# Moving the start addresses of staged weights and activations in one fp32r network kernel

## The chip, the cores and the metric

One core of one Trainium2 chip runs the whole program. The metric is the device time of one execution in microseconds; of several runs the median is given, with the lowest and the highest.

## What is computed

Two network blocks of two layers each, on 256 tokens of width 1024, all in float32. Cut to the part that the change touches most, a layer of the second block is

```
h = rmsnorm(x, norm1_g[l])
z = h @ w_in[l]                      # projections of four attentions, and 4 x 1024 gates
o = four attentions of z             # each 256 wide
lifted = einsum('bsnc,ncd->bsnd', branches, w_branch[l])
mixed = sum(sigmoid(z_gate) * lifted, over the four)
x = x + mixed @ w_out[l]
h2 = rmsnorm(x, norm2_g[l])
x = x + square(relu(h2 @ w_up[l])) @ w_down[l]      # w_up 1024 x 4096
```

The first block has a layer with attention and pooling and a layer with a gated convolution, each followed by a mixture of 16 experts. A final norm ends the program.

## The kernel before

**Products.** Activations lie transposed in SBUF: 128 features on the partitions, 256 tokens along the free dimension. A product of full precision is built from three fp32r products: a tensor is held as a high part and a low part, and `mm3` (L160 to L163) issues the high weights times the high activations (L161), the high weights times the low activations (L162) and the low weights times the high activations (L163). Each of the three loads its own 128x128 weight tile (a row LDWEIGHTS, on the weight-load side of TensorE) and then streams 256 columns (a row MATMUL). The weight load of the next product overlaps the streaming of this one.

**Staging.** Weights come by DMA as 1 MB chunks `w`. `half` (L132 to L137) takes half a chunk and has ScalarE write its high part `whi` (L133) and VectorE its low part `wlo` (L134), each 128x1024 floats, into a staging pool. The pools stand in a list and are taken in turn: `stage` alone in the first block, `stage` and `stage_b` in the second block, `stage`, `stage_b` and `ml` during its feed-forward. So one half chunk feeds 24 products in a row (8 tiles of 128 columns, three products each), and the next 24 read their weights from the next pool of the list.

**The streamed operands.** `feature_linear` (48 products, two half chunks) streams `a` in the first block, `act` (the normed x, L1100) for the projections and gates of the second, `mx` (the mixed gates) for `w_out`, and the tag `oT` for the feed-forward's `up`. `lift` streams `oT`, the attentions' outputs. `down` streams `hid`, the squared relu, and adds into four PSUM accumulators `d`. The feed-forward has 16 steps; step cj issues `up(cj + 1)` and then `down(cj)`.

**Where tiles begin.** A pool is a stretch of each partition's SBUF, and a tile begins where the tiles allocated before it in its pool end. So an extra tile ahead of others moves all that follow. The program before has one such tile already: `gap`, 32 floats (L1632), in the pool `ml` ahead of the buffers of `hid`.

**Order.** Each engine has its own instruction stream, in an order that a scheduler sets when the program is built. VectorE (DVE) computes in its stream the low parts of the weights, the low parts of activations, the residual adds, the masks and the softmax pieces. The branch of the fourth attention finds its largest scores with eight rounds of MAX and MATCH_REPLACE for each of two token blocks (L1369 to L1373), through a small tile `m8`.

Of the kernel before, what the change touches and what calls it, by code (L numbers as in the profile page):

```python
# [10 lines left out]
F32 = mybir.dt.float32  # L11
# [10 lines left out]
NK = 8  # L22
# [38 lines left out]
def build(tc, I, O):  # L61
    nc = tc.nc
    V, A, G, T = nc.vector, nc.scalar, nc.gpsimd, nc.tensor
    es = ExitStack()
    with es:
        const = es.enter_context(tc.tile_pool(name="const", bufs=1))
        ring = es.enter_context(tc.tile_pool(name="ring", bufs=4))
        stage = es.enter_context(tc.tile_pool(name="stage", bufs=1))
        psum = es.enter_context(tc.tile_pool(name="psum", bufs=1, space=PSUM))

        def acc(name="acc"):
            return psum.tile([128, 512], F32, name=name, tag="acc", bufs=2)

# [16 lines left out]
        def C(name):  # L90
            if name in C1T:
                a, n = C1T[name]
                return cst1[:, a:a + n]
            a, n = CT[name]
            return cst[:, a:a + n]
# [5 lines left out]
        b1 = ExitStack()  # L101
        c1 = b1.enter_context(tc.tile_pool(name="c1", bufs=1))
        ring_b = b1.enter_context(tc.tile_pool(name="ring_b", bufs=7))
        pb = c1.tile([128, NPB], F32, name="pb")
        cst1 = c1.tile([128, NC1], F32, name="cst1")

# [2 lines left out]
            return pb[:, a:a + n]  # L109

        ident, ones = C("ident"), C("ones")
        epst = const.tile([128, 16], F32, name="epst")[:, 0:1]
        V.memset(epst, EPS)
        identb, causal, cmpm, hsel = cb[:, 0:128], cb[:, 128:256], cb[:, 256:286], cb[:, 286:798]

# [49 lines left out]
        def pair(shape, name, pool, bufs=1):  # L165
            return (pool.tile(shape, F32R, name=name + "h", tag=name + "h", bufs=bufs),
                    pool.tile(shape, F32R, name=name + "l", tag=name + "l", bufs=bufs))

        def token_linear(name, j0, a, done, ncol=512, alloc=acc, between=lambda: None, need=None):

            blocks = (0, 1)
# [29 lines left out]
        def feature_linear(name, j, a):  # L201

            w = chunk2(name, j)
            ps = acc("fm")
            for mm in range(2):
                for k in range(NK):
                    mm3(ps[:, S * mm:S * mm + S], tile_of(w[mm], k), pick(a, lambda z: z[:, k]),
                        k == 0, k == NK - 1)
            return ps
# [147 lines left out]
        class Conditions:  # L357
# [3 lines left out]
            def __init__(self, small, alloc=acc):  # L361
                self.small, self.ps, self.blocks, self.alloc = small, None, [], alloc
# [58 lines left out]
        def moe(layer, norm, rc, work, blocks):  # L421
# [180 lines left out]
                                 skip_group_check=True)  # L602
                return yg[0]

            g2 = const.tile([128, NK], F32, name=f"g2_{layer}")

            def collect(m):
                residual(m, ys[m // 2][:, S * (m % 2):S * (m % 2) + S], g2[:, m:m + 1])
# [391 lines left out]
        with tc.tile_pool(name="l1", bufs=1) as wk:  # L1000
# [36 lines left out]
            for part in range(4):  # L1037
                for cj in range(2):
# [3 lines left out]
                    if part in (0, 3):  # L1042
                        f = wk.tile([128, 2, S], F32, name="mf", tag="mf", bufs=2)
# [34 lines left out]
def block2(tc, I, O, E):  # L1078
    nc = tc.nc
    V, A, G, T = nc.vector, nc.scalar, nc.gpsimd, nc.tensor  # L1080
    const, ring, xT = E["const"], E["ring"], E["xT"]
# [5 lines left out]

    with ExitStack() as es:
        wk = es.enter_context(tc.tile_pool(name="b2", bufs=1))

        cosT, sinT = E["trig"][:, 0], E["trig"][:, 1]

# [27 lines left out]
        for l in range(2):  # L1120
# [6 lines left out]
            oT = pair([128, 8, S], "oT", wk)  # L1127
            ph = ExitStack()
            at = ph.enter_context(tc.tile_pool(name=f"at{l}", bufs=1))
            def scaled(out, ps, b, eng):  # L1130
                if eng is A:
                    A.activation(out, ps, AF.Copy, scale=scales[0][:, b:b + 1])
                else:
                    V.tensor_scalar(out, ps, scales[0][:, b:b + 1], None, op0=ALU.mult)
# [231 lines left out]
            def best(b):  # L1366
                s0, s1 = (0, 128) if b == 0 else (128, 384)
                src = sc[:, s0:s1]
                for r in range(8):  # L1369
                    m8 = at.tile([128, 8], F32, name="m8", tag="m8", bufs=2)  # L1370
                    V.max(m8, src)
                    V.match_replace(scw[:, s0:s1], m8, src, -3.0e38)
                    src = scw[:, s0:s1]  # L1373
                n_ = s1 - s0
                kp = at.tile([128, S], F32, name="kp", tag="rl", bufs=2)
                V.tensor_tensor(kp[:, :n_], scw[:, s0:s1], sc[:, s0:s1], op=ALU.is_equal)
                V.scalar_tensor_tensor(dmask[:, s1 - 128:s1], kp[:, n_ - 128:n_], NEG, causal, op0=ALU.mult,
                                       op1=ALU.add)
                if b:
                    V.tensor_scalar(dmask[:, s0:s1 - 128], kp[:, :n_ - 128], NEG, None, op0=ALU.mult)  # L1380
# [236 lines left out]
            ph.close()  # L1617
            ph = ExitStack()
            ml = ph.enter_context(tc.tile_pool(name=f"ml{l}", bufs=1))
            E["stages"].append(ml)  # L1620
            dn = [sps("d0"), sps("d1"), sps("d2"), tps("d3")]
            hid = {}

            def up(cj):
                ps = feature_linear(f"up{l}", cj, a)
                hr = ml.tile([128, 2, S], F32, name="hr", tag="hr", bufs=2)
                hf = hr.rearrange("p m t -> p (m t)")
                A.activation(hf, ps, AF.Relu)
                V.tensor_tensor(hf, hf, hf, op=ALU.mult)
                hid[cj] = pair([128, 2, S], "hid", ml, bufs=2)  # L1630
                if cj == 0:
                    V.memset(ml.tile([128, 32], F32, name="gap", tag="gap"), 0.0)  # L1632
                split(hr, hid[cj][0], hid[cj][1])

            def down(cj):
# [223 lines left out]
```

## Time and profile before

| | us |
|---|---|
| median of 3 runs | 1513.59 |
| lowest, highest | 1512.26, 1514.64 |
| the profiled execution, its own time | 1514.41 |
| its span, first to last instruction | 1512.7 |

The span is what all times of the trace count from. The profile gives busy time by engine, groups of equal instructions with their mean duration, and the instructions in order of time. A TensorE row's duration goes from the start of a product to the end of its last column's way through the array, so that durations of successive products overlap; what a product costs in a dense stretch is the distance from its start to the next one's start, called its pitch here. A window that begins at the start of one product and ends at the start of the 24th product after it is 24 pitches long. The count in brackets in such a window includes products that reach into it, so it is some 2 or 3 above 24, and at places below that where a record is missing.

### The profile page before, as it was taken

To read this page: it belongs to the slowest core of one execution; us is meant where nothing else is said; L and a number is where in the kernel's file an instruction comes from. 1 tells how busy PE (TensorE), PEld (TensorE's weight loads), DVE (VectorE), ACT (ScalarE), POOL (GpSimd) and SP (SyncE) were. 2 spreads that over 40 slices of the span, in tenths; PEclk is the share of its full clock that TensorE was granted. 3 is DMA by queue.
4 is the path that set the end of the run, shared out by engine and by line. 5 is a ranking of instruction groups with operands and counts; after the bars stand their busy time and mean duration, and the time that the engine had idled before them with its cause. 6 is when DMAs were issued, how large, how long until landed. Compare 5 with 4: busy or idle time off the path is not lost.

```text
span 1512.7 us, 25576 instructions
## 1 busy us (share of the span) xinstructions
PE 1474.8 (97%) x10412; PEld 1178.0 (78%) x10412; DVE 857.9 (57%) x1682; ACT 658.1 (44%) x1114; POOL 26.7 (2%) x59
## 2 busy tenths in 40 slices
PE   8999899989999999899999999999999999999998
PEld 3756645445986444698789999999898789999998
DVE  2765452225646222657777775555758777765554
ACT  2544311115433111556564554444565654654443
POOL 0000000000000000010000000000010000000000
PEclk9999999999999999999999999999999999999999
DMA  9974789739584986553315464554444135465540
GB/s 396 388 296 167 304 368 404 292 136 371 205 349 174 414 336 246 178 171 116 136 59 186 177 221 175 188 196 167 136 157 168 57 114 184 177 223 179 185 166 29
DMA packets 47005, 324.85 MB, mean 215 GB/s; under 512 B 5600, under 2 KB 5984, under 8 KB 8480
## 3 DMA queue, kind: packets, MB, share of 16 engines
q1 hardware_dynamic: 45360, 320.12, 55.8%
q8 instruction: 86, 1.41, 0.4%
q10 hardware_dynamic: 1296, 1.55, 0.3%
q0 software_dynamic: 224, 1.46, 0.3%
q14 instruction: 39, 0.32, 0.1%
HBM read 322.06 MB, written 1.05 MB: 214 GB/s over the span
## 4 chain that ended last, share of the span: by engine, by line
PE 56%; DVE 2%; ACT 1%; issue 0%; DVEq 0%; ACTq 0%
PE fm L162 10%; PE fm L163 10%; PE fm L161 10%; PE d L162 4%; PE d L161 4%; PE d L163 4%; PE tm L194 1%; PE tm L195 1%; PE tm L196 1%; PE sp L1486 1%; PE lf L162 1%; PE lf L163 1%; PE lf L161 1%; PE po L1475 1%; PE ptp L1469 1%; DVE sc L1359 1%
## 5 line engine op out<-in xcount | busy, mean ns | idle before, releaser
L134 DVE TENSOR_TENSOR wlo<-w,whi 128x1024 fp32r<-128x1024 f32 (+1 forms) x314 | 378.4, 1208 | 251.9 <-ACT whi L133 249.2
L133 ACT CAST whi<-w 128x1024 fp32r<-128x1024 f32 (+1 forms) x314 | 324.3, 1035 | 384.5 <-PE fm L162 230.7
L161 PE MATMUL fm<-acth,whi 128*128 128x256 f32 x592 | 169.4, 286 | 0.0
L162 PE MATMUL fm<-actl,whi 128*128 128x256 f32 x592 | 168.3, 284 | 0.0
L163 PE MATMUL fm<-acth,wlo 128*128 128x256 f32 x592 | 167.9, 284 | 0.0
L163 PE MATMUL d<-hidh,wlo 128*128 128x256 f32 x512 | 144.2, 282 | 0.0
L162 PE MATMUL d<-hidl,whi 128*128 128x256 f32 x512 | 144.0, 281 | 0.0
L161 PE MATMUL d<-hidh,whi 128*128 128x256 f32 x512 | 143.9, 281 | 0.0
L162 PE MATMUL fm<-oTl,whi 128*128 128x256 f32 x512 | 143.6, 281 | 0.0
L163 PE MATMUL fm<-oTh,wlo 128*128 128x256 f32 x512 | 143.3, 280 | 0.0
L161 PE MATMUL fm<-oTh,whi 128*128 128x256 f32 x512 | 143.1, 280 | 0.0
L162 PEld LDWEIGHTS fm<-actl,whi 128*128 128x128 f32 x592 | 112.5, 190 | 2.3 <-issue 2.3
L161 PEld LDWEIGHTS fm<-acth,whi 128*128 128x128 f32 x592 | 113.2, 191 | 1.0 <-issue 0.8
L163 PEld LDWEIGHTS fm<-acth,wlo 128*128 128x128 f32 x592 | 112.4, 190 | 1.3 <-issue 1.0
L162 PEld LDWEIGHTS fm<-oTl,whi 128*128 128x128 f32 x512 | 96.8, 189 | 0.4 <-DVE oTl L1100 0.4
L162 PEld LDWEIGHTS d<-hidl,whi 128*128 128x128 f32 x512 | 96.7, 189 | 0.4 <-DVE hidl L134 0.4
L161 PEld LDWEIGHTS fm<-oTh,whi 128*128 128x128 f32 x512 | 96.9, 190 | 0.0
L161 PEld LDWEIGHTS d<-hidh,whi 128*128 128x128 f32 x512 | 96.8, 189 | 0.1
L163 PEld LDWEIGHTS d<-hidh,wlo 128*128 128x128 f32 x512 | 96.7, 189 | 0.1
L163 PEld LDWEIGHTS fm<-oTh,wlo 128*128 128x128 f32 x512 | 96.7, 189 | 0.0
L590 PE MATMUL yp<-w,ht 128*64 128x512 f32 x272 | 84.1, 646 | 6.8 <-PEq L774 3.5
L557 PE MATMUL gu<-w,xg 128*64 128x512 f32 x288 | 70.1, 599 | 0.0
(537 smaller groups left out, 2904.5 us busy)
## 6 DMA issues: line engine op xcount, KB each, us to landing
w<-gu SPq DMA_DIRECT2D x64, 1024.0 KB, 9.3
w<-mod SPq DMA_DIRECT2D x48, 1024.0 KB, 11.2
w<-dn SPq DMA_DIRECT2D x32, 1024.0 KB, 9.7
w<-gw SPq DMA_DIRECT2D x32, 1024.0 KB, 4.8
w<-up SPq DMA_DIRECT2D x32, 1024.0 KB, 4.8
w<-dw SPq DMA_DIRECT2D x32, 1024.0 KB, 4.8
w<-tm SPq DMA_DIRECT2D x12, 1024.0 KB, 5.0
w<-oin SPq DMA_DIRECT2D x8, 1024.0 KB, 8.3
```

The costliest lines, as they stand in the source:

```text
L133: A.copy(hi, src)
L134: V.tensor_sub(lo, src, hi.bitcast(F32))
L161: T.matmul(out, ws[0], xs[0], start=first, stop=False, skip_group_check=skip)
L162: T.matmul(out, ws[0], xs[1], start=False, stop=False, skip_group_check=skip)
L163: T.matmul(out, ws[1], xs[0], start=False, stop=last, skip_group_check=skip)
L194: T.matmul(ps, at[0], ww[0], start=first, stop=False, skip_group_check=True)
L195: T.matmul(ps, at[1], ww[0], start=False, stop=False, skip_group_check=True)
L196: T.matmul(ps, at[0], ww[1], start=False, stop=k == NK - 1, skip_group_check=True)
L557: T.matmul(gu[64 * e:64 * e + 64, :], x_[:, 4 * h + k, s0 + 64 * e:s0 + 64 * e + 64], w[e][:, 512 * k:512 * k + 512], start=(h == 0 and k ...
L590: T.matmul(yp[64 * e:64 * e + 64, :], ht[:, 128 * k + 64 * e:128 * k + 64 * e + 64], wd[e][:, 1024 * k + 512 * q:1024 * k + 512 * q + 512] ...
L1359: V.scalar_tensor_tensor(dst, rl[:, :nk], iw[:, b, h:h + 1], dst, op0=ALU.mult, op1=ALU.add)
L1469: T.transpose(tp[:, 128 * c:128 * c + 128], prs[g][:, 128 * c:128 * c + 128], ident)
```

## The change

Four small tiles are added that nobody reads, each cleared once by VectorE through the new helper `apart`: 16 floats at the head of the pool `c1` (first block), 16 at the head of `b2` (second block), 8 at the head of the attention pool `at0` and `at1`, 48 at the head of `ml0` and `ml1`. The tile `gap` in `ml` goes from 32 to 48 floats, `epst` in the constants from 16 to 8. The gate vector `g2` of the two layers of the first block becomes one tile in place of two, and `m8` has one buffer in place of two. No product, no DMA and no other shape changes.

```
--- before.py
+++ after.py
@@ -68,6 +68,10 @@
         stage = es.enter_context(tc.tile_pool(name="stage", bufs=1))
         psum = es.enter_context(tc.tile_pool(name="psum", bufs=1, space=PSUM))
 
+        def apart(pool, n):
+
+            V.memset(pool.tile([128, n], F32, name=f"gap{n}", tag=f"gap{n}"), 0.0)
+
         def acc(name="acc"):
             return psum.tile([128, 512], F32, name=name, tag="acc", bufs=2)
 
@@ -101,6 +105,7 @@
         b1 = ExitStack()
         c1 = b1.enter_context(tc.tile_pool(name="c1", bufs=1))
         ring_b = b1.enter_context(tc.tile_pool(name="ring_b", bufs=7))
+        apart(c1, 16)
         pb = c1.tile([128, NPB], F32, name="pb")
         cst1 = c1.tile([128, NC1], F32, name="cst1")
 
@@ -109,7 +114,7 @@
             return pb[:, a:a + n]
 
         ident, ones = C("ident"), C("ones")
-        epst = const.tile([128, 16], F32, name="epst")[:, 0:1]
+        epst = const.tile([128, 8], F32, name="epst")[:, 0:1]
         V.memset(epst, EPS)
         identb, causal, cmpm, hsel = cb[:, 0:128], cb[:, 128:256], cb[:, 256:286], cb[:, 286:798]
 
@@ -602,7 +607,7 @@
                                  skip_group_check=True)
                 return yg[0]
 
-            g2 = const.tile([128, NK], F32, name=f"g2_{layer}")
+            g2 = const.tile([128, NK], F32, name="g2", tag="g2")
 
             def collect(m):
                 residual(m, ys[m // 2][:, S * (m % 2):S * (m % 2) + S], g2[:, m:m + 1])
@@ -1087,6 +1092,7 @@
 
     with ExitStack() as es:
         wk = es.enter_context(tc.tile_pool(name="b2", bufs=1))
+        E["apart"](wk, 16)
 
         cosT, sinT = E["trig"][:, 0], E["trig"][:, 1]
 
@@ -1127,6 +1133,7 @@
             oT = pair([128, 8, S], "oT", wk)
             ph = ExitStack()
             at = ph.enter_context(tc.tile_pool(name=f"at{l}", bufs=1))
+            E["apart"](at, 8)
             def scaled(out, ps, b, eng):
                 if eng is A:
                     A.activation(out, ps, AF.Copy, scale=scales[0][:, b:b + 1])
@@ -1367,7 +1374,7 @@
                 s0, s1 = (0, 128) if b == 0 else (128, 384)
                 src = sc[:, s0:s1]
                 for r in range(8):
-                    m8 = at.tile([128, 8], F32, name="m8", tag="m8", bufs=2)
+                    m8 = at.tile([128, 8], F32, name="m8", tag="m8")
                     V.max(m8, src)
                     V.match_replace(scw[:, s0:s1], m8, src, -3.0e38)
                     src = scw[:, s0:s1]
@@ -1617,6 +1624,7 @@
             ph.close()
             ph = ExitStack()
             ml = ph.enter_context(tc.tile_pool(name=f"ml{l}", bufs=1))
+            E["apart"](ml, 48)
             E["stages"].append(ml)
             dn = [sps("d0"), sps("d1"), sps("d2"), tps("d3")]
             hid = {}
@@ -1629,7 +1637,7 @@
                 V.tensor_tensor(hf, hf, hf, op=ALU.mult)
                 hid[cj] = pair([128, 2, S], "hid", ml, bufs=2)
                 if cj == 0:
-                    V.memset(ml.tile([128, 32], F32, name="gap", tag="gap"), 0.0)
+                    V.memset(ml.tile([128, 48], F32, name="gap", tag="gap"), 0.0)
                 split(hr, hid[cj][0], hid[cj][1])
 
             def down(cj):
```

The addresses of the built program show what moves. Given is each tile's start modulo 256 bytes in its partition; all tiles of 128 weight columns and all 256-column operands of one tensor share it, as their strides are multiples of 512 bytes.

| tile | before | after |
|---|---|---|
| weights of `stage` | 0 | 192 |
| weights of `stage_b` | 64 | 64 |
| weights of `ml` | 192 | 192 |
| streamed `a`, `act`, `oT` | 0 | 0 |
| streamed `hid` | 64 | 0 |
| streamed `mx` | 64 | 96 |
| streamed `mix` | 32 | 32 |

The phase of a pair, as used below, is the start of the weight tile that is loaded next minus the start of the operand that is streamed meanwhile, modulo 256 bytes. Over the 6,995 places in the executed program where one 256-column fp32r product follows another, the phases stand as follows.

| phase | 0 | 32 | 64 | 96 | 128 | 160 | 192 | 224 |
|---|---|---|---|---|---|---|---|---|
| before | 3021 | 6 | 1606 | 242 | 526 | 6 | 1158 | 430 |
| after | 6 | 32 | 2225 | 428 | 6 | 436 | 3690 | 198 |

Of the 3,021 pairs at phase 0, 914 stream `act`, 182 `oT` in `lift`, 526 `oT` in `up` and 568 `a`, and go to 192; 528 stream `hid` and go to 64; 192 stream `mx` and go to 224. The others are few. Of the rest, 524 pairs of `hid` go from 128 to 192, 192 of `mx` from 192 to 96, and 188 of `mix` and 242 of the experts' gathers from 224 to 160. In between stand the pairs that stay at 64: 900 of `act`, 180 of `lift` and 528 of `up`. In `token_linear` the weights are the streamed operand, 512 columns wide; there 432 products in all have other phases than before.

In the feed-forward, twelve runs of 24 products make a period: `down` `up` `up` `down` and so on, two half chunks each, with the three pools in turn. Beginning with a second half of `down`, their phases are

| run | 1 | 2 | 3 | 4 | 5 | 6 | 7 | 8 | 9 | 10 | 11 | 12 |
|---|---|---|---|---|---|---|---|---|---|---|---|---|
| operand | hid | oT | oT | hid | hid | oT | oT | hid | hid | oT | oT | hid |
| before | 192 | 64 | 192 | 192 | 0 | 192 | 0 | 0 | 128 | 0 | 64 | 128 |
| after | 192 | 64 | 192 | 192 | 64 | 192 | 192 | 64 | 192 | 192 | 64 | 192 |

VectorE's stream at the start of the second block, before: `ygl` are the low parts of the last experts' output, `xT` the residual, `actl` the low part of the normed x, and the three branches end the loop over experts.

```order
L776 UNCONDITIONAL_BRANCH x2
L774 UNCONDITIONAL_BRANCH
L772 UNCONDITIONAL_BRANCH
L596 SCALAR_TENSOR_TENSOR ygl<-yp,cws,ygh 128x512
L418 SCALAR_TENSOR_TENSOR xT<-y_4579,g_1_4583,xT 128x256
L134 TENSOR_TENSOR wlo<-w,whi 128x1024
L596 SCALAR_TENSOR_TENSOR ygl<-yp,cws,ygh 128x512
L1100 SCALAR_TENSOR_TENSOR actl<-xT,pf,acth 128x256
L418 SCALAR_TENSOR_TENSOR xT<-y_4579,g_1_4583,xT 128x256
L134 TENSOR_TENSOR wlo<-w,whi 128x1024
L1100 SCALAR_TENSOR_TENSOR actl<-xT,pf,acth 128x256
L418 SCALAR_TENSOR_TENSOR xT<-y_4580,g_1_4583,xT 128x256 x2
```

The same place now:

```order
L781 UNCONDITIONAL_BRANCH x2
L779 UNCONDITIONAL_BRANCH
L777 UNCONDITIONAL_BRANCH
L73 MEMSET gap_6349 128x16
L601 SCALAR_TENSOR_TENSOR ygl<-yp,cws,ygh 128x512
L423 SCALAR_TENSOR_TENSOR xT<-y_4581,g_4585,xT 128x256
L139 TENSOR_TENSOR wlo<-w,whi 128x1024
L601 SCALAR_TENSOR_TENSOR ygl<-yp,cws,ygh 128x512
L1106 SCALAR_TENSOR_TENSOR actl<-xT,pf,acth 128x256
L423 SCALAR_TENSOR_TENSOR xT<-y_4581,g_4585,xT 128x256
L139 TENSOR_TENSOR wlo<-w,whi 128x1024
L73 MEMSET gap_6363 128x8
```

The 16-float tile's clear stands ahead of `ygl` behind the branches, and the 8-float tile's clear behind the second `wlo`.

VectorE's stream at the start of the feed-forward, before: `xT` adds the last product of `w_out`, `oTl` is the low part of the normed x.

```order
L134 TENSOR_TENSOR wlo<-w,whi 128x1024
L1100 SCALAR_TENSOR_TENSOR oTl<-xT,pf,oTh 128x256 x2
L134 TENSOR_TENSOR wlo<-w,whi 128x1024
L1610 TENSOR_TENSOR xT<-fm,xT 128x512
L1632 MEMSET gap 128x32
L134 TENSOR_TENSOR wlo<-w,whi 128x1024
L1100 SCALAR_TENSOR_TENSOR oTl<-xT,pf,oTh 128x256 x2
```

The same place now:

```order
L139 TENSOR_TENSOR wlo<-w,whi 128x1024
L1106 SCALAR_TENSOR_TENSOR oTl<-xT,pf,oTh 128x256 x2
L139 TENSOR_TENSOR wlo<-w,whi 128x1024
L1617 TENSOR_TENSOR xT<-fm,xT 128x512
L73 MEMSET gap_9327 128x48
L1640 MEMSET gap 128x48
L139 TENSOR_TENSOR wlo<-w,whi 128x1024
L1106 SCALAR_TENSOR_TENSOR oTl<-xT,pf,oTh 128x256 x2
```

A second clear stands ahead of the one that was there.

VectorE's stream in the fourth attention's search, at the step from the first token block (128 wide) to the second (256 wide), before; `kp` and `dmask` make the first block's mask, `kcm` belongs to another attention.

```order
L1371 MAX m_7715<-scw 128x8
L1371 MAX m_7721<-sc 128x8
L1372 MATCH_REPLACE scw<-m_7715,scw 128x128
L1198 TENSOR_TENSOR gt<-fm,rstd 128x512
L1376 TENSOR_TENSOR kp<-scw,sc 128x128
L1421 COPY kcm<-cmp 64x16
L1422 COPY kcm<-cmp 64x16
L134 TENSOR_TENSOR wlo<-w,whi 128x1024
L1377 SCALAR_TENSOR_TENSOR dmask<-kp,cb 128x128
L1372 MATCH_REPLACE scw<-m_7721,sc 128x256
```

The same place now:

```order
L1378 MAX m_7721<-scw 128x8
L1379 MATCH_REPLACE scw<-m_7721,scw 128x128
L1383 TENSOR_TENSOR kp<-scw,sc 128x128
L1205 TENSOR_TENSOR gt<-fm,rstd 128x512
L1384 SCALAR_TENSOR_TENSOR dmask<-kp,cb 128x128
L1428 COPY kcm<-cmp 64x16
L1429 COPY kcm<-cmp 64x16
L139 TENSOR_TENSOR wlo<-w,whi 128x1024
L1378 MAX m_7727<-sc 128x8
L1379 MATCH_REPLACE scw<-m_7727,sc 128x256
```

The MAX of the second block no longer stands ahead of the last MATCH_REPLACE of the first, but behind the mask.

## Rows read from the trace of the kernel before

**Rows 1.** The page: busy time, granted clock in 40 slices, chain by engine.

```profile
PE 1474.8 (97%) x10412; PEld 1178.0 (78%) x10412; DVE 857.9 (57%) x1682; ACT 658.1 (44%) x1114; POOL 26.7 (2%) x59
...
PEclk9999999999999999999999999999999999999999
...
PE 56%; DVE 2%; ACT 1%; issue 0%; DVEq 0%; ACTq 0%
```

**Rows 2.** Groups by line and shape: busy us, mean ns, idle before.

```profile
L161 PE MATMUL fm<-acth,whi 128*128 128x256 f32 x592 | 169.4, 286 | 0.0
```

**Rows 3.** Windows of TensorE, one feed-forward period: length, busy, clock, DMA, GB/s.

```profile
949.32:952.15 2.83, 2.83 (x26) 1.00 0.72 240
952.15:954.89 2.74, 2.74 (x27) 1.00 0.32 135
954.89:957.61 2.72, 2.72 (x27) 1.00 0.62 208
957.61:960.33 2.72, 2.72 (x27) 1.00 0.45 184
960.33:963.21 2.88, 2.88 (x27) 1.00 0.69 230
963.21:966.03 2.82, 2.82 (x27) 1.00 0.33 137
966.03:968.90 2.87, 2.87 (x27) 1.00 0.73 231
968.90:971.77 2.87, 2.87 (x27) 1.00 0.32 134
971.77:974.61 2.84, 2.84 (x27) 1.00 0.81 239
974.61:977.48 2.87, 2.87 (x26) 1.00 0.32 134
977.48:980.31 2.83, 2.83 (x26) 1.00 0.70 272
980.31:983.16 2.85, 2.85 (x26) 1.00 0.24 98
sum 33.84, PE 33.84; mean PE 2.82
```

**Rows 4.** Windows of TensorE elsewhere, each from one start to another.

```profile
384.08:422.64 38.56, 38.56 (x323) 1.00 0.52 182
433.59:444.41 10.82, 10.82 (x94) 1.00 1.01 426
801.95:804.78 2.83, 2.83 (x27) 1.00 0.81 339
804.78:807.66 2.88, 2.88 (x27) 1.00 0.83 262
868.13:870.95 2.82, 2.82 (x26) 1.00 0.49 142
1301.24:1303.96 2.72, 2.72 (x26) 1.00 0.82 334
```

**Rows 5.** Windows of TensorE: an attention stretch, a feed-forward stretch.

```profile
650.00:880.00 230.00, 228.65 (x1835) 1.00 0.40 143
885.40:1053.67 168.27, 168.27 (x1428) 1.00 0.53 191
```

**Rows 6.** Timeline of VectorE, three places: start, duration, instruction, idle before.

```profile
612.16 0.75 DVE L596 SCALAR_TENSOR_TENSOR ygl<-yp,cws,ygh 128x512 fp32r<-128x512 f32 x1 [8.55 <-ACT ygh L595]
...
617.66 1.22 DVE L134 TENSOR_TENSOR wlo<-w,whi 128x1024 fp32r<-128x1024 f32 x1
...
877.39 0.09 DVE L1632 MEMSET gap<- 128x32 f32 x1
```

**Rows 7.** Timeline of VectorE in the fourth attention's search.

```profile
712.93 0.28 DVE L1371 MAX8 m<-scw 128x8 f32<-128x128 f32 x1
...
713.32 0.28 DVE L1372 MATCH_REPLACE8 scw<-m,scw 128x128 f32<-128x128 f32 x1
```

More of the change, by code (lines that the diff above doesn't have):

```diff
@@ L69, in build, with apart @@
         psum = es.enter_context(tc.tile_pool(name="psum", bufs=1, space=PSUM))
+        def apart(pool, n):
+            V.memset(pool.tile([128, n], F32, name=f"gap{n}", tag=f"gap{n}"), 0.0)
         def acc(name="acc"):
@@ L103, in build @@
         ring_b = b1.enter_context(tc.tile_pool(name="ring_b", bufs=7))
+        apart(c1, 16)
         pb = c1.tile([128, NPB], F32, name="pb")
@@ L111, in build @@
         ident, ones = C("ident"), C("ones")
-        epst = const.tile([128, 16], F32, name="epst")[:, 0:1]
+        epst = const.tile([128, 8], F32, name="epst")[:, 0:1]
         V.memset(epst, EPS)
@@ L603, in down @@
                 return yg[0]
-            g2 = const.tile([128, NK], F32, name=f"g2_{layer}")
+            g2 = const.tile([128, NK], F32, name="g2", tag="g2")
             def collect(m):
@@ L1089, in block2 @@
         wk = es.enter_context(tc.tile_pool(name="b2", bufs=1))
+        E["apart"](wk, 16)
         cosT, sinT = E["trig"][:, 0], E["trig"][:, 1]
@@ L1129, in block2 @@
             at = ph.enter_context(tc.tile_pool(name=f"at{l}", bufs=1))
+            E["apart"](at, 8)
             def scaled(out, ps, b, eng):
@@ L1369, in best @@
                 for r in range(8):
-                    m8 = at.tile([128, 8], F32, name="m8", tag="m8", bufs=2)
+                    m8 = at.tile([128, 8], F32, name="m8", tag="m8")
                     V.max(m8, src)
@@ L1619, in block2 @@
             ml = ph.enter_context(tc.tile_pool(name=f"ml{l}", bufs=1))
+            E["apart"](ml, 48)
             E["stages"].append(ml)
@@ L1631, in up @@
                 if cj == 0:
-                    V.memset(ml.tile([128, 32], F32, name="gap", tag="gap"), 0.0)
+                    V.memset(ml.tile([128, 48], F32, name="gap", tag="gap"), 0.0)
                 split(hr, hid[cj][0], hid[cj][1])
```

## The prediction

> **What bounds the kernel.** I read the page first. TensorE is busy 97% of the span at a granted clock of nine tenths or more in every slice, and of the chain that ended last 56% lies on TensorE and 2% on VectorE, the next engine [rows 1]. So the end moves with what a product costs on TensorE. The groups by line then show that the 256-column products are the largest part, and that products of one shape and type differ: 286 ns mean for one group, 282 for another [rows 2]. A mean mixes cases, so I went to windows: a run of 24 products read from one staging tile, from its first start to the start behind it. The window's length over 24 is the pitch. The reader is to see that lengths of 2.72, 2.83 and 2.88 us stand side by side in one feed-forward period, all at clock 1.00 [rows 3].
>
> Laid beside the table of phases, the twelve windows of the period sort themselves. The four runs at phase 0 (windows 5, 7, 8, 10) take 2.88, 2.87, 2.87 and 2.87 us, 120.0 to 119.6 ns a product. The two at 128 (windows 9 and 12) take 2.84 and 2.85, some 118.5 ns. The six at 64 or 192 take 2.83, 2.74, 2.72, 2.72, 2.82 and 2.83 us. These six have two paces: a slow one of 2.83 us (117.9 ns) and a quick one of 2.72 us (113.3 ns). The quick one began inside window 2 and held over three tensors and pools until a run at phase 0 ended it; behind such a run comes the slow pace. Elsewhere it is alike: a run of `act` at 64 takes 2.83 us, the next one at 0 takes 2.88; `mx` at 192 takes 2.82 us in the first layer and 2.72 in the second [rows 4].
>
> Is it the phase, or the pool? With `hid` streamed, `stage` is at 192 and runs at 2.72 to 2.83 us while `stage_b` is at 0 and takes 2.88; with `oT` streamed the same pools change places, `stage` at 0 takes 2.87 and `stage_b` at 64 takes 2.74 and 2.83 [rows 3]. So phase 0 is what the slow windows share. The load of the next weights runs beside the streaming, and whether the two begin at one phase is all that differs.
>
> A rule speaks against that. The Trainium skill, page "TensorE: Matmul & The Clock Gate", section "Step-by-step: what each phase is for", says that TensorE reads streamed operand and weights through two independent ports, and that loading the next weights takes no bandwidth from the running product. By it the start addresses could not matter and the sum below would be nothing. The trace differs: equal products take 113.3, 117.9 or 120.0 ns with their phase [rows 3]. I follow the rows.
>
> **What the change adds up to.** All terms are prices per product times the counts in the change's tables.
>
> The feed-forward is the largest. It is 16 `up` and 16 `down` of two halves in each of two layers, 128 runs or 10.67 periods, and dense: TensorE is busy in all 168.27 us of the stretch shown [rows 5]. So each nanosecond of pitch there is one of the end. A period takes 33.84 us [rows 3]. After the change all twelve runs are at 64 or 192. If the mixture of the paces stays that of the six runs which are there already (together 16.66 us), a period takes 33.32 us: 0.52 saved, times 10.67 gives 5.5 us. The bounds: with all twelve slow, 33.96 us, a loss of 1.3 us in all, because the three quick windows would be lost; with all twelve quick, 32.64 us, a gain of 12.8.
>
> In projections, gates and `lift`, 1,096 pairs leave phase 0 at 120.0 ns, and 1,080 pairs at 64 stand between them at 117.9 [rows 4]. With no run at phase 0 left, nothing ends the quick pace there either, but `act` shows no quick window of its own, so I take 116.8 ns, midway between the slow pace and the feed-forward's mixture of 115.7 (16.66 us over 144). That is 1,096 x 3.2 = 3.5 us and 1,080 x 1.1 = 1.2 us. The bounds are 2.3 us (all slow) and 7.3 + 5.0 = 12.3 us (all quick).
>
> The first block's `a`, 568 pairs in stretches at 120.5 ns with some waits in them [rows 4], goes from 0 to 192: at the same 3.2 ns, 1.8 us; bounds 1.2 and 3.8.
>
> `mx`: 192 pairs go from 0 to 224. The nearest row is `mix`, which runs at 224 now: 92 products in 10.82 us, 117.6 ns [rows 4], so 0.5 us. The other 192 go from 192 (115.4 ns over both layers) to 96, for which no row has a price; between 113.3 and 120.0 it is from -0.4 to +0.9 us, and I take 117.6 as at 224, 0.4 us lost. Together 0.1 us gained. The 430 pairs that go from 224 to 160 have no price either: from -1.8 to +1.0 us, taken as nothing, since neither end phase is a multiple of 64. The same holds of the 432 wide products of `token_linear`: by the largest step in the rows, 6.7 ns, at most 2.9 us either way, taken as nothing.
>
> Sum of the gains: 5.5 + 3.5 + 1.2 + 1.8 + 0.1 = 12.1 us.
>
> The costs. A clear of 32 floats takes 0.09 us [rows 6]. The 16-float one at the second block's start stands ahead of a `ygl` for which VectorE waits 8.55 us idle [rows 6], so it is hidden as long as what it waits for (earlier users of that memory) is done. The 8-float one of the first layer stands behind the `wlo` at 617.66 us, in a stretch where VectorE has no idle time, so it counts; that of the second layer and the two of 48 floats too at most: 4 x 0.09, some 0.3 us. The one `m8`: MAX of a round needs the MATCH_REPLACE of the round before through `scw` anyway, they follow each other as at 712.93 and 713.32 us [rows 7]. Only the second block's first MAX is later, behind the mask and not ahead of it: the mask comes earlier by one MAX, the search ends where it did. Nothing counted. The shared `g2` and the smaller `epst` issue nothing new.
>
> Last, in the attentions some of the quicker products will only wait longer. TensorE is idle 1.35 us of the 230 us shown there [rows 5], so little is lost; I take 0.5 us for both layers.
>
> Net 12.1 - 0.3 - 0.5 = 11.3 us. The profiled execution took 1514.41 us, 0.8 above the median; 11.3 off the median of 1513.59 gives **1502.3 us**.
>
> **Rivals.**
> 1. *All slow.* Every run at 64 or 192 settles at 117.9 ns. For it: each such run behind a phase 0 run has that pace. Against it: those that start without such a run before them are often quick, and windows 2 to 4 keep it over three boundaries [rows 3]. The feed-forward loses 1.3, projections gain 2.3, `a` 1.2, `mx` about 0.1, clears cost 0.3: 2.0 gained, 1511.6 us. That is within 0.2% (3.0 us), about what a measurement of this kernel can tell from no change.
> 2. *All quick.* Nothing ends the quick pace any more, and it holds everywhere: 12.8 + 12.3 + 3.8 - 0.8 = 28.1 us gained, 1485.5 us. For it: only runs at 0 ended it inside the period. Against it: `mx` at 192 kept the slow pace for whole runs in the first layer [rows 4], and phases 64 and 192 still change with each half chunk.
> 3. *No effect.* Something other than the phase makes the pace, for example what else reads SBUF at that point of the period. The windows recur with the period and the DMA share differs between them, but two at 2.87 us have shares of 0.73 and 0.32 [rows 3], so that is weak. Then only the clears count: 1513.9 us. The rule of two ports that the Trainium skill states on "TensorE: Matmul & The Clock Gate" ("Step-by-step: what each phase is for") would lead here too.
> 4. *Slower, by a wait on VectorE.* The clear of 8 floats in the first layer takes memory that the first block has just given up, and waits for the experts' last products and loads. If one of these ends late, the low parts `actl` and `wlo` behind it in VectorE's stream stand, and TensorE's first products of the second block behind them, one for one. It decides from a wait of 14.3 us on (11.3 of gain and 3.0); with 15 us the time is 1517. Against it: the last product of that memory's users is the residual's, which the add just ahead of the clear waits for too.
>
> **How the numbers follow.** The mixture 0.68, all quick 0.17, all slow 0.09, no effect 0.03, a wait 0.03. The mixture alone, with 30% to 65% of the runs quick, the terms without a row included, spans 1495 to 1508. The range from 1487 to 1511 adds the cases between it and the two pure paces, and leaves out about half of each of these, no effect and the wait: some 0.19. Faster by over 0.2% are the mixture and all quick, 0.85; within it all slow and no effect, 0.12; slower 0.03.
>
> **What would show it.** In the feed-forward no window of 24 products longer than 2.84 us, a period of 32.6 to 33.9 us against 33.84; runs of `act` alternating between 192 and 64 with equal lengths; the mean of the `act` group well below 286 ns. If runs at 64 or 192 still take 2.88 us, the phase was not the cause and the prediction fails at its first step. If all are 2.83, it fails at the mixture, and so it does if all are 2.72. The clears should show as four rows of VectorE of about 0.09 us with no idle time ahead of them that TensorE then repeats.

## The result and the profile after

| | before | after |
|---|---|---|
| median, us | 1513.23 (6 runs) | 1498.05 (6 runs) |
| lowest, highest | 1511.98, 1515.65 | 1494.53, 1499.67 |
| the profiled execution | 1514.41 | 1494.53 |
| its span | 1512.7 | 1492.8 |

The ratio is 0.9895, with a 95% interval of 0.9883 to 0.9907: 15.9 us less, between 14.1 and 17.7 of 1513.23. 1502.3 us with a range from 1487 to 1511 was predicted, 11.3 us less. The two profiled executions lie further apart, 19.9 us of span, since the one of after is the fastest of its six; what is read below of a stretch is read from these two.

The page of the changed kernel, the lines that answer to [rows 1] and [rows 2] (line numbers are up to 8 higher):

```profile
PE 1451.6 (97%) x10410; PEld 1154.5 (77%) x10412; DVE 858.0 (57%) x1688; ACT 658.1 (44%) x1114; POOL 27.2 (2%) x59
...
PEclk9999999999999999999999999999999999999999
...
PE 52%; DVE 5%; ACT 1%; issue 1%; DVEq 0%; ACTq 0%
...
L166 PE MATMUL fm<-acth,whi 128*128 128x256 f32 x592 | 166.9, 282 | 0.0
```

TensorE is as full as before, at the same granted clock, and is busy for 23.2 us less; the other engines' busy time is what it was. The mean of the `act` products fell from 286 to 282 ns. (The 282 ns that the prediction names for the kernel before is another row's, that of `d<-hidh,wlo`, L163.) VectorE's share of the chain rose from 2% to 5%. That would fit quicker products which meet the staging of weights a little more often, but no run tests it.

Windows of TensorE after the change: a dense feed-forward stretch of each layer, cut at the same products as the 168.27 us of [rows 5], and inside the first the four runs before 912.75 us and the twelve from there on.

```profile
880.17:1043.31 163.14, 163.04 (x1429) 1.00 0.54 197
1312.85:1475.98 163.13, 163.13 (x1428) 1.00 0.47 167
901.44:912.75 11.31, 11.31 (x99) 1.00 0.44 154
912.75:945.39 32.64, 32.64 (x291) 1.00 0.54 192
```

The four runs up to 912.75 take 11.31 us, 117.8 ns a product. The twelve from there on take 32.64 us where [rows 3] had 33.84: 113.3 ns in every one of them, at 64 and at 192 alike, and so on to the end of the layer. The second layer turns at the same place of its program. Of the table of twelve runs it is run 2, `oT` at 64 behind `hid` at 192: the run in which every period of the kernel before turned quick too, as the second window of [rows 3], 2.74 us, shows. There a run at phase 0 ended the quick pace three runs later; here nothing does.

Windows elsewhere after the change, which answer to [rows 4]: `a`, `mix`, two runs of `act` (64 and 192), another of `act` at 192, `mx` at 96 and at 224.

```profile
382.07:419.94 37.87, 37.87 (x324) 1.00 0.54 191
430.89:442.01 11.12, 11.12 (x94) 1.00 1.01 426
...
798.39:801.11 2.72, 2.72 (x27) 1.00 0.79 325
801.11:803.83 2.72, 2.72 (x27) 1.00 0.83 259
708.90:711.73 2.83, 2.83 (x27) 1.00 0.21 38
862.97:865.82 2.85, 2.85 (x26) 1.00 0.53 141
865.82:868.62 2.80, 2.80 (x26) 1.00 0.65 275
```

Neighbouring `act` runs that took 2.83 and 2.88 us take 2.72 each. Others, as the fifth window, stay at the slow pace of 2.83 in this execution. What went to a phase that is no multiple of 64 got nothing or lost: `mix` takes 11.12 us for 92 products in place of 10.82, and `mx` takes 2.85 us at 96, where it took 2.82 or 2.72 at 192.

VectorE's timeline at the two clears of the second block's start, and the line of the helper:

```profile
606.53 0.07 DVE L73 MEMSET gap<- 128x16 f32 x1 [3.66 <-PEq L777]
611.24 0.75 DVE L601 SCALAR_TENSOR_TENSOR ygl<-yp,cws,ygh 128x512 fp32r<-128x512 f32 x1 [4.63 <-ACT ygh L600]
...
615.83 1.22 DVE L139 TENSOR_TENSOR wlo<-w,whi 128x1024 fp32r<-128x1024 f32 x1
616.98 0.48 DVE L1106 SCALAR_TENSOR_TENSOR actl<-xT,pf,acth 128x256 fp32r<-128x256 f32 x1
617.00 0.07 DVE L73 MEMSET gap<- 128x8 f32 x1
617.37 0.87 DVE L423 SCALAR_TENSOR_TENSOR xT<-y,g,xT 128x256 f32<-128x256 f32 x2
...
L73 DVE MEMSET gap<- x6: 65/72/98, 0.9 to 1304.9; 128x16 f32 x2, 128x8 f32 x2, 128x48 f32 x2
```

The 16-float clear lies inside the idle time ahead of `ygl`, the 8-float one takes 0.07 us and VectorE does not wait at it; the six clears together are under 0.6 us.

### The profile page after: what moved, and what is told of

Same layout as the page of the kernel before. It is cut to its first block, busy times and chain, and to the rows that moved or that the text cites. A ratio compares the mean times of both kernels' runs of the same rounds, so it can differ in the third digit from the quotient of the medians.

```text
span 1492.8 us, 25584 instructions
## 1 busy us (share of the span) xinstructions
PE 1451.6 (97%) x10410; PEld 1154.5 (77%) x10412; DVE 858.0 (57%) x1688; ACT 658.1 (44%) x1114; POOL 27.2 (2%) x59
## 4 chain that ended last, share of the span: by engine, by line
PE 52%; DVE 5%; ACT 1%; issue 1%; DVEq 0%; ACTq 0%
PE fm L167 9%; PE fm L166 9%; PE fm L168 9%; PE d L167 4%; PE d L166 4%; PE d L168 4%; DVE wlo L139 2%; PE tm L200 1%; PE tm L201 1%; PE tm L199 1%; PE sp L1493 1%; PE po L1482 1%; PE ptp L1476 1%; PE lf L167 1%; PE lf L168 1%; PE lf L166 1%
```

## The experiments

Phases are counted over the 6,995 places where one 256-column fp32r product follows another. Most kernels below change only tile sizes. Edits are shown against the changed kernel and cut to the rows that matter; `...` stands for what is left out of a row. Where it says so, `rstd` has one buffer in place of two, which makes 1 KB of room. "Quick" is 113.3 ns a product, "slow" 117.8.

**1. All of the change but the phases.**

```
-        apart(c1, 16)
-        epst = const.tile([128, 8], F32, name="epst")[:, 0:1]
+        spare = const.tile([128, 24], F32, name="epst")
+        epst = spare[:, 0:1]
-        E["apart"](wk, 16)
+        V.memset(E["spare"][:, 8:24], 0.0)
-            E["apart"](at, 8)
+            V.memset(E["spare"][:, 8:16], 0.0)
-            E["apart"](ml, 48)
+            E["apart"](ml, 64)
-  ... ml.tile([128, 48], F32, name="gap", tag="gap") ...
+  ... ml.tile([128, 32], F32, name="gap", tag="gap") ...
```

> All else of the change is kept (shared g2, one m8, the clears of the second block, the order that follows), but the added tiles are sized so that every phase is as before: 3,021 pairs at 0, 526 at 128. Theory (the phase sets the pitch): the time of before, 1513 us, within 2. Rival (something else in the change, its order or the one m8, brought the gain): 1498 us.

Measured: 1513.8 us, ratio 1.0008 (0.9994 to 1.0021). With the phases of before the gain is gone. The one `m8`, the shared `g2`, the clears and the other order of some rows are worth nothing that shows.

**2. Everything at phase 0.** `epst` 24 floats, no tile at the head of `c1`, `b2`, `at` and `ml`, 24 floats (two buffers) ahead in `stage_b`, `gap` 64, one buffer of `rstd`.

```
+        E["apart"](stage_b, 24)
-  ... ml.tile([128, 48], F32, name="gap", tag="gap") ...
+  ... ml.tile([128, 64], F32, name="gap", tag="gap") ...
```

> All three staging pools and all operands of the second block start at 0 modulo 256, so that 6,299 pairs have phase 0. Theory: a feed-forward period takes 12 x 2.88 = 34.56 us against 33.84, 7.7 us more in all; the runs of act and lift that were at 64 lose 1,080 x 2.1 ns = 2.3 us, mx at 192 about 0.8: about 1524 us. Rival (the position in the period, not the phase, makes the pitch): 1513 us.

Measured: 1523.69 us, ratio 1.006 (1.0037 to 1.0083). With twice as many pairs at 0 it is slower by about what the rows said, 5.6 to 12.6 us; the 6,288 products of `a`, `act`, `oT`, `mx` and `hid` there have a median pitch of 120 ns.

**3. The staging pool `stage` alone.**

```
-            E["apart"](at, 8)
-            E["apart"](ml, 48)
-  ... ml.tile([128, 48], F32, name="gap", tag="gap") ...
+  ... ml.tile([128, 32], F32, name="gap", tag="gap") ...
```

> Only the constants and the two 16-float tiles are as in the change: the weights of stage go from 0 to 192; hid stays at 64 and mx at 64, so that hid runs at 128, 0, 128 and mx at 128 and 0. Theory: projections, lift and a gain (up to 12.3 and 3.8 us if all quick, 3.5 if all slow), the feed-forward stays near 33.8 us a period: 1500 to 1509 us. Rival (the gain is the feed-forward's alone): 1513 us.

Measured: 1506.19 us, ratio 0.9953 (0.994 to 0.9966), 7.1 us less. Its windows: a run of `act`, and a feed-forward period.

```profile
798.55:801.27 2.72, 2.72 (x26) 1.00 0.14 39
...
949.51:983.30 33.79, 33.79 (x290) 1.00 0.52 186
```

`act` is quick, while the feed-forward, with `hid` now at 128, 0 and 128, takes 33.79 us a period. Summed from start to start, `act`, `lift` and `a` together take 8.8 us less than before here, and 8.4 less with the whole change; `up` and `down` take 0.9 less here, and 11.0 less with the whole change. So a little under half of the change's gain is the projections' and the first block's, the rest the feed-forward's.

**4. Everything at 192.** 16 floats (two buffers) ahead in `stage_b`, `at` and `ml`, one buffer of `rstd`.

```
+        E["apart"](stage_b, 16)
-            E["apart"](at, 8)
+            E["apart"](at, 16)
-            E["apart"](ml, 48)
+            E["apart"](ml, 16)
```

> All three staging pools start at 192 and all operands of the second block at 0, so that 6,206 pairs have phase 192 and no run ends at a change of phase. If any phase but 0 and 128 lets the quick pace hold once it has begun: feed-forward periods of 32.64 us and mx at 113 to 118 ns, 1494 to 1499 us. Rival (the quick pace is begun by a run at 64 that follows one at 192, as the trace after the change shows it at 912.75 us, and cannot begin between runs at 192): feed-forward periods of 33.9 us, about 1510 us.

Measured: 1512.95 us, ratio 0.9998 (0.9984 to 1.0013). No pair of the second block is at 0, and nothing is gained. Windows of its trace: a stretch of `act`, and the feed-forward of each layer.

```profile
800.79:823.40 22.61, 22.61 (x194) 1.00 0.53 187
922.10:1052.12 130.02, 130.02 (x1106) 1.00 0.50 181
1362.56:1492.59 130.03, 130.03 (x1106) 1.00 0.45 157
```

192 products in 22.61 us and 1,104 in 130.02 are 117.8 ns each: the slow pace everywhere in the second block. This is the first rival of the prediction, to within 1.4 us, on a layout of its own. Leaving phase 0 alone is not what the change gains by; the quick pace is.

**5. 192 once more, and 192 at other addresses.** The same kernel again, and one with weights at 0 and operands at 64:

```
-        apart(c1, 16)
-        epst = const.tile([128, 8], F32, name="epst")[:, 0:1]
+        epst = const.tile([128, 24], F32, name="epst")[:, 0:1]
```

> The run with all at 192 once more, one look. If the slow pace there is a matter of the place and not of chance: again 117.8 ns in all the feed-forward. If each execution draws its pace behind the waits: quick stretches in one layer or both, each worth some 6 us.

> Every pair of the second block at 192 again, but with all weights at 0 and all operands at 64, so that only the absolute addresses differ from the earlier run at 192; a in the first block is back at 0. If the difference (the phase) sets what a stretch can do: no quick run in the second block, feed-forward stretches at 117.8 ns, 1511 to 1517 us. If it was the absolute address, or chance: quick stretches as in the run with all at 64, 1495 to 1500 us.

Measured: 1511.51 us in one run; 1511.27 us, ratio 0.9986 (0.9972 to 1.0000). Both feed-forwards are slow throughout in both. In the second kernel, a stretch of `act` and 153 products of `mx`; in the first kernel, the same 37 products of `a` (first block, 192) in the execution of experiment 4 and in this one:

```profile
795.97:818.58 22.61, 22.61 (x194) 1.00 0.53 184
857.80:875.14 17.34, 17.34 (x154) 1.00 0.59 214
...
135.54:139.73 4.19, 4.19 (x38) 1.00 0.01 4
...
136.24:140.60 4.36, 4.36 (x39) 1.00 0.01 4
```

For the feed-forward it is the difference of the addresses that counts, not where they lie, and it came out the same in all three executions. But 192 alone can be quick too: the `mx` shown takes 113.3 ns a product, and so do 239 products near the end of that kernel's second layer. And the pace behind a wait does differ between executions of one kernel: the 37 products of `a` took 113.3 ns in one and 117.8 in the other. Of the 30 stretches of over 12 products between waits (starts under 170 ns apart) in the second block, none was quick in the execution of experiment 4, two short ones in the repeat, and two, the long ones named, in the second kernel. Inside a stretch the pace never turned.

**6. Everything at 64.** Weights at 192, operands of the second block at 128, one buffer of `rstd`.

```
-        E["apart"](wk, 16)
+        E["apart"](wk, 48)
-            E["apart"](at, 8)
+            E["apart"](at, 48)
-  ... ml.tile([128, 48], F32, name="gap", tag="gap") ...
+  ... ml.tile([128, 80], F32, name="gap", tag="gap") ...
```

> All three staging pools start at 192 and all operands of the second block at 128, so that 5,731 pairs of the second block have phase 64 and none changes it; a in the first block stays at 192. Theory (the quick pace is begun where runs at 192 and 64 meet): no quick run in the second block, feed-forward periods of 33.9 us, 1510 to 1514 us. Rival (64 in itself is a quick phase): feed-forward periods of 32.6 us, 1495 to 1500 us.

Measured: 1495.2 us, ratio 0.9872 (0.9842 to 0.9902). The theory after experiment 4, that runs at 192 and 64 have to meet, fell: there is no 192 here in the second block. The windows: `act` of the first layer, its feed-forward, `act` of the second layer.

```profile
797.35:819.11 21.76, 21.76 (x195) 1.00 0.57 191
910.24:1040.80 130.56, 130.56 (x1155) 1.00 0.54 190
1228.76:1251.38 22.62, 22.62 (x195) 1.00 0.53 186
```

The same 192 products take 21.76 us in one layer and 22.62 in the other, and the feed-forward's 1,152 are quick. At 64 both paces occur, each held until a wait, or once a single pitch of 122 ns in place of 113 (824.77 us); at 192 alone it is nearly always the slow one. Of the same 30 stretches 18 were quick here, so with one phase throughout, what counts is how often a wait leaves the quick pace behind. The feed-forward's gain hangs on one such wait in each layer, and this kernel was traced once; its four executions took 1489.69 to 1498.85 us, all below the lowest of before beside them, 1509.40.

**7. A sweep of phases in the feed-forward.** The weights go through one pool of four padded buffers, and each half chunk takes an offset from a list.

```
+            if phases:
+                ph_, pl_ = [(p + 64) % 256 // 4 for p in phases.pop(0)]
+                hi = sp_.tile([128, 1088], F32R, name="whi", tag="whi", bufs=4)[:, ph_:ph_ + 1024]
+                lo = sp_.tile([128, 1088], F32R, name="wlo", tag="wlo", bufs=4)[:, pl_:pl_ + 1024]
```

> The change's kernel with the feed-forward's weights staged in one pool of four padded buffers, so that each run of 24 products has a phase of its own choice: in the first layer 0, p, p for p from 16 to 240 in steps of 16, in the second 0, 192, p, and at the end some other sequences. Theory: only phase 0 gives 120.0 ns; 64 and 192 give 117.8 behind a run at 0 in the first layer; in the second a run at 64 behind one at 192 comes quick (113.3). For the other phases the rows so far give 118.5 at 128, 117 at 224, 119 at 96 and 120 to 121 at 160. Rival (the period is not 256 bytes but shorter or longer): 128 would look like 0, or all below 256 would look alike.

Measured: 1505.61 us in one run. Windows of the first layer, each of two runs (48 products) behind a run at 0: 192, 64, 128, 160, 224; then single runs at 0, 192 and 64, and 64 and 192 behind a 0. Last, of the second layer, 64 and 240 behind a quick run at 192.

```profile
978.10:983.54 5.44, 5.44 (x50) 1.00 0.46 161
909.55:915.21 5.66, 5.66 (x51) 1.00 0.55 184
943.80:949.49 5.69, 5.69 (x50) 1.00 0.50 174
960.93:966.68 5.75, 5.75 (x51) 1.00 0.49 181
994.89:1000.50 5.61, 5.61 (x50) 1.00 0.51 181
1020.48:1023.36 2.88, 2.88 (x27) 1.00 0.79 253
1023.36:1026.08 2.72, 2.72 (x27) 1.00 0.28 118
1026.08:1028.80 2.72, 2.72 (x27) 1.00 0.67 220
1012.00:1014.83 2.83, 2.83 (x26) 1.00 0.28 116
1014.83:1017.66 2.83, 2.83 (x27) 1.00 0.70 240
1349.72:1352.44 2.72, 2.72 (x27) 1.00 0.71 217
1442.31:1445.13 2.82, 2.82 (x27) 1.00 0.36 145
```

| phase | 0 | 16 | 32 | 48 | 64 | 80 | 96 | 112 |
|---|---|---|---|---|---|---|---|---|
| ns a product | 119.8 | 118.3 | 118.3 | 118.5 | 117.9 | 118.8 | 117.3 | 119.8 |

| phase | 128 | 144 | 160 | 176 | 192 | 208 | 224 | 240 |
|---|---|---|---|---|---|---|---|---|
| ns a product | 118.5 | 118.3 | 119.8 | 118.1 | 113.3 | 116.9 | 116.9 | 120.0 |

(The length of the two runs behind a 0, over 48; at 48 bytes of the second run alone, as the first had a wait; at 0 the mean over its runs.) The period is not shorter than 256 bytes, as 128 does not look like 0. Phase 0 is not alone either: 112, 160 and 240 take 119.8 to 120.0. What stands out is 192, which starts quick behind a run at 0 every time here (once a wait ended it), and 64, which behind a run at 0 is slow, but quick behind a quick 192. In a row, 0, 64, 192 is slow, slow, slow; 0, 192, 64 is slow, quick, quick. In the second layer, behind a quick run at 192, only 64 and 192 stay quick; the others take 116.5 to 119.6 ns, 240 among them 117.5 where it took 120.0 behind a 0. And a 192 behind a 224 is slow, while a 64 behind a 160 turns quick within its first six products (114.3 ns over the run). Which pace a run has depends on what it follows.

**8. High and low weights at different phases.** The same lists with two phases a run.

> As the sweep, but the high and the low weights of a run have different phases; behind two runs at (0, 0) come six at (0, 64), (64, 0), (0, 192), (192, 0), (64, 192), (192, 64), (0, 128). A product's own weights are loaded while the product before it streams. Theory (the load of the next weights against the streaming of this product): with the high part at 0 and the low at 64 the first and the third of each three products are slow (120), the second is quicker. Rival (the product's own weights against its own operand): the first and the second are slow, the third is quicker.

Measured: 1505.96 us in one run. From start to start in the first layer, over six runs each, in ns, the first, second and third of each three products:

| high, low | 0, 64 | 64, 0 | 0, 192 | 192, 0 | 64, 192 | 192, 64 | 0, 128 |
|---|---|---|---|---|---|---|---|
| first | 117.9 | 118.3 | 119.4 | 115.2 | 113.1 | 113.0 | 119.1 |
| second | 117.4 | 117.7 | 120.7 | 117.3 | 114.1 | 114.0 | 119.2 |
| third | 118.5 | 117.4 | 113.3 | 120.8 | 113.1 | 113.0 | 119.2 |

Neither theory fits all of it. With (0, 192) the first and second are slow and the third quick, which is what the rival said (own weights, own operand), and (192, 0) leans the same way; but with (0, 64) no product takes 120 though two of three have phase 0 by the rival, and two of three by mine. The timeline at (0, 192), starts on TensorE:

```profile
935.21 0.28 PE L175 MATMUL d<-hidh,whi 128*128 128x256 f32 x1
935.33 0.28 PE L176 MATMUL d<-hidl,whi 128*128 128x256 f32 x1
935.45 0.28 PE L177 MATMUL d<-hidh,wlo 128*128 128x256 f32 x1
935.56 0.28 PE L175 MATMUL d<-hidh,whi 128*128 128x256 f32 x1
```

0.12, 0.12, 0.11 us. What is settled: a third of the products at 64 or 192 in place of 0 is enough to bring the mean of the three from 120.0 to 117.8 or 117.9 (at 128 only to 119.2), and 64 and 192 within each three are quick in both layers.

**9. Versions beyond the change.** With `mx`, `mix` and the experts' gathers at 64 or 192 too (24 floats ahead in `l1`, `m0` and `m1`, 48 in `at`, one buffer of `rstd`); the change once more; and the change with `mx` at 0 (16 floats ahead in `at`), 16 floats ahead in `ml`, and 32 floats between the high and the low weights in `stage_b` and `ml`.

```
+            if sp_ is not stage and sp_ not in parted:
+                parted.append(sp_)
+                sp_.tile([128, 32], F32, name="part", tag="part", bufs=1)
```

> As the change, but mx, mix and the experts' gathers are moved too, so that 6,729 of the 6,995 pairs are at 64 or 192 (mx 192 and 64, mix and gathers 64); one buffer of rstd in place of two makes the room. Theory: mx goes from 118.8 and 116.7 to 113.3 ns, 384 x 4.5 = 1.7 us; mix and gathers from 120.9 to 117.8, 430 x 3 = 1.3 us: 1495 us, 3 under the change. Rival (what stays at 64 behind no run at 192 is no better than 160 and 224): 1497 to 1498 us.

> The changed kernel once more. If the quick pace begins at a place of the program (192 before 64), nearly all of the feed-forward is quick again and the time lies at 1494 to 1500 us. If it begins by chance, the feed-forward of this execution has another share of quick runs, and the times spread more than those of before.

> As the change, with mx at 0 too, but in stage_b the high weights are at 64 and the low at 192, and in ml the high at 192 and the low at 64; stage stays at 192. Theory: 192 and 64 meet within every three products, so the quick pace begins at once behind each wait: the attention stretches and the first period of the feed-forward gain up to 3 us over the change and mx 1.7: 1491 to 1495 us. Rival (what is still slow there waits for weights): as the change, 1494 to 1498 us.

Measured: 1494.26 us, ratio 0.9862 (0.9843 to 0.9881); the change again 1493.94 us, ratio 0.988 (0.9858 to 0.9903); 1493.48 us, ratio 0.9877 (0.9858 to 0.9896). The three can't be told apart. Their traces show the part that was meant (`mx` at 113.3 ns but for its first products and one run), 1.1 and 1.4 us summed over its starts, which is less than these runs can resolve. In the first one `mix` took 12.87 us in the stretch that answers to the 11.12 us above. In two parts:

```profile
432.83:437.87 5.04, 5.04 (x24) 0.50 1.02 432
437.87:445.70 7.83, 7.83 (x70) 1.00 1.00 421
```

Behind 16 products of 20 columns (430.26 to 432.83 us) the granted clock was 0.50, the lower of its two levels (1.2 and 2.4 GHz), for 24 products of some 210 ns; in the trace of after it was 1.00 throughout. At 1.00 the other 69 products, at 64 now, took 113.5 ns a product, and the two shorter stretches of `mix` behind them 117.8 and 113.6, where 160 takes 120.0: the move paid there too. Such stretches of the lower clock lie in different places of the first block from one execution to the next. In the traces of this study the second block's first 256-column products start anywhere between 649 and 656 us, and the times follow: the kernel of experiment 4 reaches that product at 656.1 us in one execution and at 651.9 in the other, with spans of 1515.3 and 1509.8 us.

The change again, a run of `act` that took 2.83 us in the trace of after, and the first twelve quick runs of the feed-forward:

```profile
708.08:710.80 2.72, 2.72 (x26) 1.00 0.23 42
912.54:945.18 32.64, 32.64 (x290) 1.00 0.53 190
```

The feed-forward was quick from the same place on in both layers, as the first theory had it. In the attentions, where waits lie between the stretches, some had another pace than before. So in the changed kernel there are two ways into the quick pace. One is a wait, behind which executions differ. The other is a change of phase without a wait: wherever the second block's pace turned from slow to quick without one, in both traces of this kernel, a run at 64 began there behind a run at 192 or 96. Not every such run turns: at 904.27 us in after, `oT` at 64 behind `oT` at 192 stays slow.

## Why the prediction held, and where it was off

**The first step, that the phase sets the pitch,** is shown: all else of the change without the phases gives nothing (experiment 1), more of phase 0 gives a loss (2), and part of the change gives part of the gain (3). The third rival, no effect, is out. TensorE reads the streamed operand and the weights through two independent ports, as the Trainium skill says on "TensorE: Matmul & The Clock Gate", section "Step-by-step: what each phase is for". That did not make the addresses indifferent here, as the prediction took the rule to say: the pitch went from 113.3 to 120.0 ns at one clock, by addresses alone. Whether the two reads meet at a port, or elsewhere, no run shows.

**The step that was mis-sized is the mixture of the paces.** "If the mixture of the paces stays that of the six runs which are there already" gave 5.5 us for the feed-forward. In place of 33.32 us a period it takes 32.64 once the quick pace has begun, and the dense stretches went from 168.27 to 163.14 and 163.13 us: 10.3 us. Summed over all starts, the 3,072 products of `up` and `down` went from 363.6 to 352.6 us, 11.0 less, near the bound of 12.8 that the prediction named for all quick. By the prediction's own sign, "it fails at the mixture, and so it does if all are 2.72", this step failed from 912.75 us on. What ended the quick pace before, the runs at phase 0, is gone, as the second rival argued. The slow runs that are left lie ahead of that place, in little more than the first period. (In passing, windows 2 to 4 of [rows 3] cross two boundaries and stream two tensors, not three as the prediction has it; it changes nothing in the sum.)

**The projections** were taken at 116.8 ns, between slow and the mixture: 3.5 and 1.2 us. By starts, `act` went from 232.4 to 226.3 us (1,872 products) and `lift` from 49.2 to 48.2 (384): 7.1 us, against 4.7 less the 0.5 for waits. The price was too small for the same reason: with no run at 0 left, more of the runs are quick than was assumed.

**The smaller terms.** `a`: 1.8 predicted, 70.1 to 68.7 us, so 1.3, nearer the slow bound; its long stretch went from 120.5 to 118.3 ns. It has no 64 among its runs, as experiment 4 has none. `mx`: 0.1 gained predicted, 0.5 lost (45.8 to 46.3 us). Its price at 192 came from one run of each layer; the next run at 192 in the first layer (873.82 us) took 2.72 us too, so before was a little quicker than [rows 4] suggest. `mix` at 160, taken as nothing, lost 0.6 (22.8 to 23.4). So did the 432 wide products of `token_linear`: where they follow each other their pitch was 229.2 ns before (229.4 in experiment 1) and 231.8 after (231.9 when the change ran again), 1.1 us in all, inside the bound of 2.9. The clears took what was said, and the 8-float one did not wait, so the fourth rival is out. Together 17.2 us of the 19.9 between the two profiles; the rest is not assigned.

**What was right by luck.** The prediction took the pace as something that only runs at phase 0 end, and priced runs at 64 and at 192 alike. Experiments 4 and 5 show that a layout with all pairs of the second block at 192, which leaves phase 0 just as the change does, gains nothing or next to it. Had the change put `stage_b` and `mx` at that phase as well, the first rival (1511.6) would have come about, as it did in experiment 4 (1512.95), and I gave it 9 in 100. In the feed-forward of the change the quick pace began where a run at 64 follows one at 192, and nothing in the prediction asked for that.

**Open.** Why the quick pace begins. In the feed-forward it begins at one place of the program (both layers, two executions of the change), where a run at 64 follows one at 192; at 192 behind 0 in the sweep though not in [rows 3], where window 6 is a 192 behind a 0 and slow; behind a wait at times, often at 64 and seldom at 192. Why some changes to 64 turn the pace and others do not is not known. Whether the weights that count are the next product's or its own is open too (experiment 8). Operands whose high and low parts have different phases were not tried.

## What to carry to other kernels

Compare start-to-start distances of equal matmuls by runs, not by group means: means of 282 and 286 ns hid pitches of 113.3, 117.8 and 120.0 ns. Where fp32r products are dense and load new weights each time, try staged weights 64 and 192 bytes behind the streamed operand modulo 256 with both occurring, or 64 alone, which rests on one trace here; avoid 0, and measure, since 192 alone brought nothing. A layout is to be tested with a control that has the same extra tiles at the old phases.

## What the runs showed that I had not expected

At one clock and one instruction form, a product has a steady rate of 113.3 or 117.8 ns that lasts for over a thousand products and that neither its shape nor its phase alone decides: at 64, 21.76 and 22.62 us for the same 192 products in two layers of one execution. And behind a run at 0, phases 112, 160 and 240 are as slow as 0, 119.8 to 120.0 ns, so that no simple distance from 0 orders them.
